# Uneven first pieces in the mixing groups and other places for the second blocks of feed-forward slabs, in one decoder layer on one core

## The chip, the cores and the metric

The kernel runs on one core of a Trainium2 chip, as one program. The metric is the device time of one execution in microseconds. Of its engines, TensorE does the matrix products (a weight load, LDWEIGHTS, and a MATMUL for each), VectorE (DVE), ScalarE (ACT) and GpSimd (POOL) work on slabs in SBUF, and SyncE (SP) issues most of the transfers. Three executions of the kernel before took 2538.45, 2538.80 and 2538.89 us, a median of 2538.8 us.

## The reference

One layer of a hybrid decoder for a prompt of 2048 tokens and for eight samples of eight tokens, all with 1024 features and the same weights. In short:

```python
def mixer(h, pos, s_ret, s_hg, w_in, ret_norm_w, hgrn_norm_w, lb, w_out):
    proj = h @ w_in                       # 1024 -> 8 * 512
    rq, rk, rv, rg, hq, hf, hi, hg = jnp.split(proj, idx, axis=-1)
    ...                                   # rotary; 4 retention heads, 4 HGRN2 heads, chunkwise
    o_r, s_ret_new = chunk_gla(rq, rk, rv, log_g_ret, s_ret)
    o_h, s_hg_new = chunk_gla(hq, k_in, v_in, log_f, s_hg)
    o = jnp.concatenate([gated(o_r), gated(o_h)], axis=-1)
    return o @ w_out, s_ret_new, s_hg_new

x = x + mixer(rmsnorm(x, norm_mix_w), ...)
h = rmsnorm(x, norm_ffn_w)
x = x + jnp.square(jax.nn.relu(h @ w_up)) @ w_down   # 1024 -> 4096 -> 1024
y = rmsnorm(x, final_norm_w)
```

Outputs are y for prompt and samples and the states of both kinds of heads.

## The kernel before

Activations lie with features on the 128 partitions and tokens along the columns. The 2112 tokens are worked off in three **mixing groups** of 640, 768 and 704 columns (`GROUPS`, L42; the last one holds the 64 sample tokens) and then in three **feed-forward groups** of 704 columns (`feed_groups`).

Every large product is made of three matmuls: weights and activations are split in a high and a low part, and hi*hi, hi*lo and lo*hi are added up in PSUM. All these matmuls are issued by the helper `matmul` (L1365 is its line). It also counts columns and drives a clock of "ticks" by them: other work (splitting weights, norms, the recurrences) is put on an agenda at a number of ticks, and is written out between the matmuls where its tick comes. A scheduler then orders the instructions of each engine by readiness and priority.

A PSUM bank holds 512 columns of float32, so a group of more than 512 columns is cut in two **pieces**, `g.pieces`. In a mixing group, `proj` goes through the weight blocks and issues, for each of the three products, one matmul for each piece, both with the same weights: first piece, second piece, first piece, and so on. So do `first_pair` for the first two projections of the kernel and `out_part` (through `proj`) for the first half of the output projection. The pieces are also the units in which results leave PSUM: `normed` (L784), `swapped` (L797, L798) and `evacuated` (L804) copy piece by piece on ScalarE, and the rotary products (L864) run on VectorE. `halves`, `parts` and `both_sums` split a slab of squares piece by piece and add it over the partitions with the weights `ones_r` (L594, L595). `parts` puts high and low part into one slab when twice the length fits into 768 columns, and takes another slab for the low part otherwise. The values (`values`) use the weights as moving operand, 256 columns at a time, and don't depend on pieces.

SBUF **slabs** are 768 columns of float32 (3072 bytes a partition) each, 49 of them in a pool. In the feed-forward stage a slab often holds two blocks of 352 columns (two rows of blocks of a half group); `pair` gives the view of it, with the second block at column 384. `out_proj` writes pairs from whole slabs of heads that are cut in two pieces of 352 columns; `up_quad` (the first eighth), `up` (seven Strassen-like products for each further eighth) and `down` read pairs as moving operand. In `up` and `down` three matmuls use one block, then three the other; in `up_quad` six and six. Pairs are also read and written by the splits (`halve`, L1409 and L1413), the sums (L1420, L1557, L1629), the squares (L1499 to L1504), the scaling of the residual and the final norm, and by transfers to and from DRAM.

The matmuls of a mixing group are interleaved with small ones of the recurrences (L992 to L1250). In a feed-forward group long runs of L1365 stand without anything between them.

Of the kernel before, what the change touches and what calls it, by code (L numbers as in the profile page):

```python
# [30 lines left out]
LAG = 14  # L31
SOON = None
SLAB = 768
NSLAB = 49
NLD = 4
NRAW, NFRAW = 4, 9
# [158 lines left out]
class Kernel:  # L195
# [25 lines left out]
    def get(self, dt=F32):  # L221
        return self.sl.tile([P, SLAB], dt, tag="slab", name="slab")

# [5 lines left out]
    def load(self):  # L229
        return self.ld.tile([P, SLAB], F32, tag="ld", name="ld")  # L230

# [199 lines left out]
    def build(self):  # L431
        nc, tc, I = self.nc, self.tc, self.I
        with ExitStack() as ctx:
            cp = ctx.enter_context(tc.tile_pool(name="cp", bufs=1))
            self.wp = ctx.enter_context(tc.tile_pool(name="wp", bufs=3))
            self.sl = ctx.enter_context(tc.tile_pool(name="sl", bufs=NSLAB))
            self.ld = ctx.enter_context(tc.tile_pool(name="ld", bufs=NLD))
# [30 lines left out]
    def groups(self, sizes):  # L468
        gs, off = [], 0
        for ns, p0, n in sizes:  # L470
            g = type("G", (), {})()
            g.i, g.ns, g.p0, g.n, g.T, g.off = len(gs), ns, p0, n, ns + n, off
            g.raw_oc, g.sources = {}, [(g, slice(0, g.T), slice(0, g.T))]
            off += g.T
            nch = n // C
            first = nch // 2
            g.pieces = [(0, g.T)] if g.T <= 512 else [(0, g.T // 2), (g.T // 2, g.T)]
            g.segs = [list(range(first)), list(range(first, nch))]
            gs.append(g)
        return gs  # L480
# [103 lines left out]
    def parts(self, src, n):  # L584

        t, half = self.getr(), SLAB // 2
        hi, lo = t[:, :n], t[:, half:half + n] if 2 * n <= SLAB else self.getr()[:, :n]
        self.nc.scalar.copy(hi, src)
# [280 lines left out]
    def values(self, g, p, b):  # L869
# [7 lines left out]
        for i0 in range(0, len(g.starts), 4):  # L877
            part = g.starts[i0:i0 + 4]
            pj = [self.bank() for _ in range(0, len(part), 2)]
            vs = [self.get() for _ in range(0, len(part), 2)]  # L880
            for i, s in enumerate(part):
                cut = slice(i % 2 * 256, i % 2 * 256 + 256)
                for kb in range(KB):
                    hh, hl = g.h[kb]
                    cols = slice((kb % 4) * 256, (kb % 4 + 1) * 256)
                    wh, wl = w[kb // 4][0][:, cols], w[kb // 4][1][:, cols]
                    for q, (a, ww) in enumerate(((hh, wh), (hh, wl), (hl, wh))):
                        self.matmul(pj[i // 2][:, cut], a[:, s:s + C], ww, start=kb == 0 and q == 0,
                                    stop=kb == KB - 1 and q == 2)
                v = vs[i // 2]  # L890
                pair = (v[:, cut.start:cut.start + P], v[:, cut.start + P:cut.stop])
                if g.ns and s == 0:
                    b["vs"], b["vrows"] = pair, v[:NS, :2 * P]
                else:
                    b["vc"].append(pair)
                if g.post:
                    with self.soon():
                        nc.scalar.activation(v[:, cut], pj[i // 2][:, cut], AF.Copy, scale=g.rc[:, i0 + i:i0 + i + 1])  # L898
                elif i % 2 or i == len(part) - 1:
                    with self.soon():  # L900
                        nc.scalar.copy(v[:, :cut.stop], pj[i // 2][:, :cut.stop])
# [457 lines left out]

    def pair(self, g, slab):  # L1360

        return slab.rearrange("p (i t) -> p i t", i=2)[:, :, :g.T // 2]

    def matmul(self, out, w, a, **k):
        self.nc.tensor.matmul(out, w, a, **k)  # L1365
# [477 lines left out]
```

## Time and profile before

| | before |
|---|---|
| median of three executions | 2538.8 us |
| profiled execution | 2538.88 us |
| its span, first to last instruction | 2537.1 us |
| TensorE matmul busy | 2506.2 us (99%) |
| VectorE busy | 1856.9 us (73%) |
| ScalarE busy | 1224.3 us (48%) |
| granted TensorE clock | 0.999 |
| read from / written to HBM | 390.62 / 138.67 MB |

The profile is of one execution. A busy share is the union of the records of an engine; a matmul's record reaches from its start to a modelled end, and records of matmuls that follow each other overlap. How fast a run of matmuls goes is therefore read from the starts: the length of an unbroken run over the number of its matmuls. The chain of work that ended last lists such runs with start, length and count. Mixing takes the first 1120 us or so of the span, the three feed-forward groups the rest, about 480 us each.

### The profile page before, as it was taken

The page shows a single profiled execution, that of the slowest core. Times are in us where ns is not written, and L with a number is a line of the kernel's source. Part 1 is how long each engine was busy: PE and PEld are TensorE (multiplying, and loading weights), DVE is VectorE, ACT ScalarE, POOL GpSimd, SP SyncE. Part 2 cuts the span into 40 slices and gives each one's busy share as a digit, 9 for nine tenths or more (in the row PEclk, how much of TensorE's full clock was granted, in tenths as well). Part 3 has the DMA queues.
Part 4 walks back from the last instruction along what each step waited for, and adds up shares of the span by engine and source line. Part 5 has one row for each costly group of instructions (what it writes and reads, how often), then busy time and mean ns, then how long its engine had stood idle before and what let it go on. Part 6 is the DMA issues. An engine that isn't in the chain of part 4 may idle for free.

```text
span 2537.1 us, 41661 instructions
## 1 busy us (share of the span) xinstructions
PE 2506.2 (99%) x16605; PEld 2480.6 (98%) x16605; DVE 1856.9 (73%) x2750; ACT 1224.3 (48%) x1769; POOL 25.1 (1%) x42
## 2 busy tenths in 40 slices
PE   8999999999999999999999999999999999999998
PEld 8999999999999999989999999999999999999998
DVE  7668866677867766656757996766699866658987
ACT  6556554345534344426444543554454445445544
POOL 0000000000000000000000000000000000000000
PEclk9999999999999999999999999999999999999999
DMA  6466685779798735484657664466766554667652
GB/s 213 150 202 235 229 295 186 237 260 313 261 338 303 267 120 172 156 297 143 195 185 255 225 204 159 152 200 184 226 230 215 175 194 154 185 193 238 206 180 70
DMA packets 209731, 532.83 MB, mean 210 GB/s; under 512 B 20736, under 2 KB 95232, under 8 KB 209536
## 3 DMA queue, kind: packets, MB, share of 16 engines
q1 hardware_dynamic: 209392, 530.14, 62.7%
q8 instruction: 131, 2.15, 0.3%
q14 instruction: 64, 0.52, 0.1%
q10 hardware_dynamic: 144, 0.02, 0.0%
HBM read 390.62 MB, written 138.67 MB: 209 GB/s over the span
## 4 chain that ended last, share of the span: by engine, by line
PE 93%; DMA 3%; DVE 3%; ACT 1%; issue 1%; SPq 0%; DVEq 0%; ACTq 0%
PE pj L1365 84%; PE mm L1062 2%; PE po L1244 1%; PE mm L1250 1%; PE mm L1119 1%; PE po L1242 1%; PE mm L595 1%; DMA raw<-w 1%; PE mm L594 1%; PE mm L1176 1%; PE po L933 1%; PE mm L992 0%; DVE slab L1023 0%; DMA s68S<-raw 0%; DMA slab<-x 0%
## 5 line engine op out<-in xcount | busy, mean ns | idle before, releaser
L1365 PE MATMUL pj<-slab,w 128*128 128x352 f32 (+2 forms) x12696 | 2115.4, 324 | 11.4 <-ACT w L648 6.5
L1365 PEld LDWEIGHTS pj<-slab,w 128*128 128x128 f32 x12696 | 2037.2, 188 | 16.3 <-ACT w L648 6.8
L338 ACT CAST w<-raw 128x1024 fp32r<-128x1024 f32 x373 | 390.7, 1048 | 620.0 <-PE pj L1365 537.1
L360 DVE TENSOR_TENSOR w<-raw,w 128x1024 fp32r<-128x1024 f32 x373 | 454.9, 1222 | 118.5 <-ACT w L338 105.7
L1365 PE MATMUL pj<-w,slab 128*128 128x256 f32 x1632 | 225.9, 288 | 0.1
L1413 DVE TENSOR_TENSOR slab<-slab 128x704 fp32r<-128x704 f32 x216 | 187.5, 885 | 32.0 <-ACT slab L1409 28.3
L1409 ACT CAST slab<-slab 128x704 fp32r<-128x704 f32 x216 | 163.6, 779 | 92.8 <-DVE slab L1420 85.8
L1365 PEld LDWEIGHTS pj<-w,slab 128*128 128x128 f32 x1632 | 205.6, 190 | 2.1 <-ACT slab L898 0.5
L1629 DVE TENSOR_TENSOR slab<-pj,slab 128x704 f32<-128x704 f32 x166 | 146.9, 888 | 65.3 <-PE pj L1365 62.7
L296 DVE TENSOR_TENSOR raw<-raw 128x1024 f32<-128x1024 f32 x60 | 73.4, 1223 | 54.6 <-DMA raw<-w 49.6
L1420 DVE TENSOR_TENSOR slab<-slab 128x704 f32<-128x704 f32 x120 | 103.6, 885 | 0.0
L1557 DVE TENSOR_TENSOR ld<-pj,slab 128x704 f32<-128x704 f32 x63 | 56.1, 890 | 55.2 <-PE pj L1365 54.9
L1043 ACT ACTIVATE slab<-slab 128x640 f32<-128x640 f32 (+2 forms) x72 | 56.2, 780 | 70.6 <-DVE slab L1039 70.2
L1557 DVE TENSOR_TENSOR slab<-pj,slab 128x704 f32<-128x704 f32 x42 | 37.4, 891 | 66.5 <-PE pj L1365 66.5
L1063 DVE COPY_PREDICATED AT<-msk,mm 128x256 f32<-128x256 uint8 (+1 forms) x72 | 38.8, 543 | 40.6 <-PE mm L1062 31.7
L413 ACT CAST slab<-slab 128x704 fp32r<-128x704 f32 (+2 forms) x48 | 36.9, 777 | 39.2 <-DMA slab<-o 16.9
L419 ACT ACTIVATE slab<-mm,eps 128x384 f32<-128x384 f32 (+3 forms) x54 | 29.5, 550 | 53.4 <-PE mm L595 50.4
L1062 PE MATMUL mm<-slab 128*128 128x128 f32 x384 | 54.1, 274 | 0.0
L1062 PEld LDWEIGHTS mm<-slab 128*128 128x128 f32 x384 | 51.1, 191 | 0.0
L1244 PE MATMUL po<-slab,S 128*128 128x128 f32 x240 | 46.3, 279 | 4.3 <-DVE S L1257 4.2
L784 ACT COPY slab<-pj 128x384 f32<-128x384 f32 (+1 forms) x64 | 26.7, 466 | 47.1 <-PE pj L1365 45.0
L1327 ACT ACTIVATE slab<-po 128x384 f32<-128x384 f32 (+2 forms) x48 | 22.0, 458 | 53.3 <-PE po L1244 53.2
(187 smaller groups left out, 1988.1 us busy)
## 6 DMA issues: line engine op xcount, KB each, us to landing
raw<-w SPq DMA_DIRECT2D x253, 512.0 KB, 4.1
u<-ld SPq DMA_DIRECT2D x96, 352.0 KB, 4.3
slab<-u SPq DMA_DIRECT2D x96, 352.0 KB, 5.2
y<-slab SPq DMA_DIRECT2D x20, 352.0 KB, 2.8
ld<-x SPq DMA_DIRECT2D x16, 384.0 KB, 6.2
raw<-s44S SPq DMA_DIRECT2D x12, 512.0 KB, 3.8
raw<-s48S SPq DMA_DIRECT2D x12, 512.0 KB, 4.4
raw<-s52S SPq DMA_DIRECT2D x12, 512.0 KB, 3.6
```

Source lines behind the costliest of these rows:

```text
L296: nc.vector.tensor_tensor(out=x[into], in0=x[a], in1=x[b], op=op)
L338: self.nc.scalar.copy(hi, raw)
L360: self.nc.vector.tensor_tensor(out=lo, in0=raw, in1=hi.bitcast(F32), op=ALU.subtract)
L1043: nc.scalar.activation(x["dd", w][:, a:T], x["dd", w][:, a:T], AF.Exp)
L1062: nc.tensor.matmul(ps[:, j * P:(j + 1) * P], qk[:, cols[c]], qk[:, cols[c]], start=True, stop=True)
L1244: nc.tensor.matmul(dst, S, qd[:, cols[c]], start=False, stop=True)
L1365: self.nc.tensor.matmul(out, w, a, **k)
L1409: self.nc.scalar.copy(self.pair(g, hi), self.pair(g, B[name]))
L1413: self.nc.vector.tensor_tensor(out=self.pair(g, lo), in0=self.pair(g, B[name]), in1=self.pair(g, hi).bitcast(F32), op=ALU.subtract)
L1420: self.nc.vector.tensor_tensor(out=self.pair(g, s), in0=self.pair(g, B[a]), in1=self.pair(g, B[b]), op=op)
L1557: nc.vector.tensor_tensor(out=b2(out), in0=ps, in1=b2(s), op=ALU.add)
L1629: nc.vector.tensor_tensor(out=r, in0=ps, in1=r, op=ALU.add)
```

## The change

Two tables of three numbers. The first piece of a mixing group is no longer half of it: 304 of 640, 400 of 768, 336 of 704 columns, so the second piece has 336, 368 and 368. And the second block of a pair slab stands at column 368 in the first feed-forward group, 360 in the second and 376 in the third, where it stood at 384 in all. The blocks stay 352 columns long. The pieces of `out_proj` are made in `feed_groups` and stay halves.

```diff
 SLAB = 768
+FIRST_PIECE = (304, 400, 336)
+SECOND_BLOCK = (368, 360, 376)
 NSLAB = 49
...
-            g.pieces = [(0, g.T)] if g.T <= 512 else [(0, g.T // 2), (g.T // 2, g.T)]
+            g.pieces = [(0, FIRST_PIECE[g.i]), (FIRST_PIECE[g.i], g.T)]
...
     def pair(self, g, slab):
 
-        return slab.rearrange("p (i t) -> p i t", i=2)[:, :, :g.T // 2]
+        return slab[:, :2 * SECOND_BLOCK[g.i]].rearrange("p (i t) -> p i t", i=2)[:, :, :g.T // 2]
```

The lines of the changed kernel stand two further down than before (L1365 is L1367 there). On TensorE in the third mixing group, between the recurrences of its third head, there stood before (line, operation, out<-in, partitions x columns, count):

```order
L594 MATMUL mm<-slab,ones_r 128x320
L595 MATMUL mm<-slab,ones_r 128x320
L1365 MATMUL pj<-slab,w 128x352 x6
L992 MATMUL mm<-con,slab 128x128 x2
L1365 MATMUL pj<-slab,w 128x352 x2
```

and now, on the same engine at the same place:

```order
L596 MATMUL mm<-slab,ones_r 128x320
L597 MATMUL mm<-slab,ones_r 128x320
L1367 MATMUL pj<-slab,w 128x368
L1367 MATMUL pj<-slab,w 128x336
L1367 MATMUL pj<-slab,w 128x368
L1367 MATMUL pj<-slab,w 128x336
L1367 MATMUL pj<-slab,w 128x368
L994 MATMUL mm<-con,slab 128x128 x2
```

The equal halves of 352 columns have become pieces of 336 and 368 in turn, and the small matmuls between them have moved by a matmul or so. On TensorE in the first feed-forward group, from the last sums of the mixing stage on, there stands now:

```order
L597 MATMUL mm<-slab,ones_r 128x384 x2
L1367 MATMUL pj<-slab,w 128x352 x812
L596 MATMUL pj<-slab,ones_r 128x352
L597 MATMUL pj<-slab,ones_r 128x352
L1367 MATMUL pj<-slab,w 128x352 x20
```

It stood there before in the same order and number (with L594, L595 and L1365), and so it does to the end of the program: in the feed-forward groups only the addresses are others. On VectorE, where the second mixing group's squares are split (L589, now L591) while the first group's heads are worked on, there stood before:

```order
L1254 COPY S<-mm 128x128 x2
L589 TENSOR_TENSOR slab<-slab 128x384 x2
L1257 SCALAR_TENSOR_TENSOR S<-S,mm 128x128
L864 TENSOR_TENSOR slab<-pj,slab 128x320
L1257 SCALAR_TENSOR_TENSOR S<-S,slab,mm 128x128
L864 TENSOR_TENSOR slab<-pj,slab 128x320
```

and now:

```order
L1256 COPY S<-mm 128x128 x2
L591 TENSOR_TENSOR slab<-slab 128x400
L1259 SCALAR_TENSOR_TENSOR S<-S,mm 128x128
L591 TENSOR_TENSOR slab<-slab 128x368
L866 TENSOR_TENSOR slab<-pj,slab 128x304
L1259 SCALAR_TENSOR_TENSOR S<-S,slab,mm 128x128
L866 TENSOR_TENSOR slab<-pj,slab 128x336
```

The state update S now stands between the two halves of the split, one place earlier.

## The prediction

> **What bounds the kernel now.** I read the page first: the span, the busy shares, and who makes up the chain that ended last.
>
> ```profile
> span 2537.1 us, 41661 instructions
> ...
> PE 2506.2 (99%) x16605; PEld 2480.6 (98%) x16605; DVE 1856.9 (73%) x2750; ACT 1224.3 (48%) x1769; POOL 25.1 (1%) x42
> ...
> PE 93%; DMA 3%; DVE 3%; ACT 1%; issue 1%; SPq 0%; DVEq 0%; ACTq 0%
> ```
>
> TensorE is the bound: 99% busy, 93% of the chain. The profiled execution took 2538.88 us, 1.8 us more than its span and within 0.1 us of the median of 2538.8; I sum against 2538.88. Next, the list of what TensorE waited for (us in total, times, longest):
>
> ```profile
> PE pj L1365 <- ACT w L648: 6.5, 2, 5.8
> PE po L1244 <- DVE S L1257: 4.2, 6, 2.0
> PE pj L1365 <- DVE slab L1660: 2.5, 2, 1.5
> ...
> PE mm L594 <- DVE slab L589: 0.5, 1, 0.5
> ```
>
> These waits are small, and the largest, on L648, is the kernel's first weights. So the time is set by how closely the matmuls of L1365 follow each other. The groups by shape give the counts:
>
> ```profile
> L1365 PE MATMUL pj<-slab,w 128*128 128x352 f32 x10056 | 1644.3, 324 | 2.6 <-DVE slab L1660 2.5
> ...
> L1365 PE MATMUL pj<-slab,w 128*128 128x384 f32 x1344 | 257.3, 340 | 1.2 <-DMA w<-w32lo 1.0 <-DMA w<-w16lo 0.2
> ```
>
> The 324 ns is the length of one record; the records overlap, so it is not the pace. The pace comes from the chain in order of time, whose rows give start, length and count of an unbroken run:
>
> ```profile
> 356.01 31.03 PE pj L1365 x179
> ...
> 751.03 25.38 PE pj L1365 x157
> ...
> 1119.84 130.93 PE pj L1365 x812
> 1254.61 346.39 PE pj L1365 x2164
> 1603.99 115.67 PE pj L1365 x716
> 1723.50 346.39 PE pj L1365 x2164
> 2072.89 115.67 PE pj L1365 x716
> 2192.40 323.52 PE pj L1365 x2022
> ```
>
> At 384 columns (second mixing group) one matmul takes 31.03/179 = 173.3 ns. At 352 columns there are **two paces**: 323.52/2022 = 160.0 ns and 346.39/2164 = 160.1 ns in the bulk of the feed-forward groups, but 25.38/157 = 161.7 ns in the third mixing group and 130.93/812 = 161.2 ns at the start of the first feed-forward group (115.67/716 = 161.6 in the next two, short waits included). One clean run of the first mixing group, from the timeline (start, length to the end of its last record, count):
>
> ```profile
> 24.19 7.20 PE L1365 MATMUL mm<-slab,w 128*128 128x320 f32 x48
> ```
>
> Less the last record (0.31 us) over 47 steps that is 146.6 ns at 320 columns. So 146.6, 160.0, 173.3 ns: 0.417 ns a column and a fixed 13.3 ns (160.0 - 352 x 0.417).
>
> **The cuts, by the slope.** A pair of pieces costs 0.417 ns times the group's columns plus twice 13.3 ns, wherever the cut lies: 304+336 = 640, 400+368 = 768, 336+368 = 704. As lengths the new pieces cost nothing. The Trainium skill's page "TensorE: Matmul & The Clock Gate", section "Back-to-back issue gap", gives the isolated warm gap as N/2.4 + 2.5 ns, 149.2 ns at 352 columns (an estimate by that page). The slope agrees with the trace, the fixed part is smaller than the 13.3 ns here; an uneven cut sums to zero by either.
>
> **The starts.** What is left of the change is where a matmul's moving operand begins. In bytes from the slab's start, the second pieces begin now at 1280, 1536 and 1408: multiples of 256 in the first two groups, 128 past one in the third. The slow 161.7 ns belongs to the third. The feed-forward pair slabs have their second block at 1536, a multiple again, and run at 160.0; but each group opens with `out_proj`, which uses whole slabs cut at 352 columns (1408 bytes), and there the slow pace returns. It then outlasts `out_proj`. The timeline shows where it ends in the first group:
>
> ```profile
> 1250.44 0.32 PE L1365 MATMUL pj<-slab,w 128*128 128x352 f32 x1
> 1250.60 0.32 PE L594 MATMUL pj<-slab,ones_r 128*128 128x352 f32 x1
> 1250.76 0.32 PE L595 MATMUL pj<-slab,ones_r 128*128 128x352 f32 x1
> 1250.92 3.20 PE L1365 MATMUL pj<-slab,w 128*128 128x352 f32 x19
> ```
>
> Two column sums with other weights break the run; behind them 19 matmuls take (3.20 - 0.32)/18 = 160.0 ns each. So I read the slow pace as a pattern in TensorE's own stream, set up where consecutive starts stand 128 bytes apart modulo 256, and kept until something breaks it. That is an inference: no matmul of L1365 in this trace starts anywhere else.
>
> - Third mixing group: as many matmuls as the second, x1344. The second piece moves from 1408 to 1344 bytes, out of the 128-byte relation. At the fast pace: 1344 x (161.66 - 160.0) = **-2.2 us**.
> - Feed-forward, the stretches at 161 ns: 812 + 716 + 716 = 2244 matmuls, less 192 of `out_proj` in each group (8 outputs x 4 units x 3 products x 2 halves), whose cut stays at 352: 1668. With the second block at 1472, 1440 or 1504 bytes I expect the pattern not to be carried on: 1668 x 1.24 = **-2.1 us**.
> - The stretches at 160.0 ns of the feed-forward and the first two mixing groups: no row shows their new starts. Ends: below, nothing excludes a gain of up to the fixed 13.3 ns a matmul; above, the slow pace, +1.66 ns. The nearest row is the 160.0 of the same instructions. I take 0.
>
> **The other engines.** They work on the same columns at other places:
>
> ```profile
> L1413 DVE TENSOR_TENSOR slab<-slab 128x704 fp32r<-128x704 f32 x216 | 187.5, 885 | 32.0 <-ACT slab L1409 28.3 <-PE pj L1365 3.2
> ...
> L414 DVE TENSOR_TENSOR slab<-slab 128x704 fp32r<-128x704 f32 x24 | 21.0, 886 | 4.3 <-ACT slab L413 4.3
> ...
> L784 ACT COPY slab<-pj 128x384 f32<-128x384 f32 x32 | 13.7, 479 | 20.7 <-PE pj L1365 19.6 <-PE po L1242 1.0
> ...
> L784 ACT COPY slab<-pj 128x352 f32<-128x352 f32 x32 | 13.0, 453 | 26.4 <-PE pj L1365 25.4 <-PE po L1242 1.0
> ```
>
> L1413 works on two blocks with a gap between them, L414 on whole slabs: 885 and 886 ns, so the gap's size costs VectorE nothing. ScalarE's L784 copies one piece out of PSUM at (479 - 453)/32 = 0.8 ns a column: 13 ns more for the longer piece, 13 less for the shorter. It hides in the idle time ahead of L784, 20.7 and 26.4 us over 32 copies each, nearly all of it waiting for TensorE; uncovered it would be 13 ns a pair. One edge: in the second group `parts` no longer fits twice 400 columns into one slab of 768 and takes another of the 49. If that made a wait, it would be at the sums behind L589, where TensorE waits 0.5 us now; I take 0, and 0.5 as its end. The scheduler moves a few small matmuls and copies by some places in the mixing groups; with the waits as short as above I give this 0, +-2 us.
>
> Sum: 2538.88 - 2.2 - 2.1 = **2534.6 us**.
>
> **Rivals.**
>
> *Starts don't matter (2538.9).* The pattern may belong to the length 352 with alternating PSUM banks, or to what precedes, and come back whatever the address. For it: the first feed-forward run stays slow long after `out_proj`, with starts that are fast later. Against it: 320 and 384 columns alternate banks too and show 146.6 and 173.3. The third group would have to stay at 161.7 as an average. The Trainium skill's page "SBUF — State Buffer", section "Who interferes with whom", says this too: TensorE has separate read ports for moving operand and weight load and never waits on anyone. The two paces of one shape, 160.0 and 161.2, are something that rule leaves out.
>
> *The pattern spreads (2550).* Now almost all matmuls start at multiples of 256 bytes; afterwards nearly every stream alternates between such a start and another one: first and second piece in all mixing groups, first and second block in the feed-forward. The one alternating stream in the trace is the slow one. If any alternation makes it: feed-forward stretches at 160.0, 2164 + 2164 + 2022 = 6350 x 1.66 = 10.5 us, first two mixing groups 2688 x 1.66 = 4.5 us, +15.0 in all; if only each changeover counts, which comes every third matmul in the feed-forward and every one in mixing, 3.5 + 4.5 = +8.0. I take the middle, 11.5: 2550.4. It makes the kernel measurably slower from 5.1/9038 = 0.56 ns a matmul on. Against it: the moves are by 32 to 96 bytes from a multiple of 256, not by 128.
>
> *The fixed 13.3 ns shrinks (2514.6).* If part of it comes from weights and moving operand starting alike, a moved start saves some. Moved starts: 3 x 672 second pieces and half of the feed-forward's pair matmuls ((192 + 1176 + 1344)/2 = 1356 a group, by the loops of `up_quad`, `up` and `down`), 6084. At all of the 13.3 ns that is 81 us; no row gives a size, and I take 4 ns, nearer to nothing: 24.3 us. Against it, a stream with other weights in the timeline:
>
> ```profile
> 750.69 0.33 PE L595 MATMUL mm<-slab,ones_r 128*128 128x384 f32 x1
> 750.87 25.38 PE L1365 MATMUL pj<-slab,w 128*128 128x352 f32 x156
> ```
>
> 0.18 us from one to the next at 384 columns: no shorter than 173.3 ns.
>
> **How the numbers follow.** About 0.2% (5.1 us) is what a measurement of this kernel can tell from no change. Forecast 0.36, starts don't matter 0.15, the pattern spreads 0.27, the fixed part shrinks 0.22. The forecast of -4.3 us, +-2 for the scheduler, lies inside the 0.2% more often than outside: 0.22 within, 0.14 faster. Faster is 0.14 + 0.22 = 0.36, same 0.22 + 0.15 = 0.37, slower 0.27. The range reaches from 2514 (the middle of the shrinking case; its further half, some 0.1, is left out) to 2552 (the dearer third of the spreading case left out). The likeliest case alone is 2532 to 2537.
>
> **What would show it.** In the chain after, the pace of the unbroken runs says all: the third mixing group's pairs at 320.0 ns instead of 323.3; the 812 and 716 runs ending faster, with the three long runs still at 160.0 (forecast); the long runs at 161 or more (spread), or below 160, and then by group, since each group has another block start (shrink). I am wrong at the root if the paces stay and the waits of TensorE change.

## The result, and the profile after

| | before | after |
|---|---|---|
| median of 18 executions each | 2538.8 us | 2542.4 us |
| ratio to before, 95% interval | | 1.0015 (1.0008 to 1.0022) |
| profiled execution / span | 2538.88 / 2537.1 us | 2543.25 / 2541.5 us |
| start of feed-forward (run x812) | 1119.84 us | 1118.71 us |
| feed-forward: start of x812 to end of x2022 | 1396.08 us | 1401.50 us |

The kernel became 0.15% slower, 3.6 us by the medians and 4.4 us by the spans. The forecast was 4.2 us faster. First the head of the page of the changed kernel, and the largest entries of its list of what TensorE waited for (us in total, times, longest):

```profile
span 2541.5 us, 41664 instructions
...
PE 2512.1 (99%) x16605; PEld 2487.5 (98%) x16605; DVE 1856.2 (73%) x2750; ACT 1221.3 (48%) x1767; POOL 25.5 (1%) x42
```

```profile
PE pj L1367 <- ACT w L650: 5.9, 1, 5.9
PE pj L1367 <- DVE slab L1662: 2.5, 2, 1.5
PE po L1246 <- DVE S L1259: 2.5, 5, 0.8
```

VectorE and ScalarE are as busy as before, and the waits are not longer in sum. One has grown by more than 0.5 us, that of L597 on L416 in the mixing groups, from 0.6 to 2.0 us; L1246 on S (L1244 before) fell by more, from 4.2 to 2.5 us. TensorE is 5.9 us busier with the same 16605 matmuls. The chain of the changed kernel in order of time (start, length, what, count) shows where:

```profile
355.29 31.16 PE pj L1367 x179
...
750.90 25.14 PE pj L1367 x157
...
1118.71 131.17 PE pj L1367 x812
1253.75 349.83 PE pj L1367 x2164
1606.58 115.57 PE pj L1367 x716
1726.02 348.69 PE pj L1367 x2164
2077.70 115.15 PE pj L1367 x716
2196.69 323.52 PE pj L1367 x2022
```

Row by row against before:

- Second mixing group (400 and 368): 31.16/179 = 174.1 ns instead of 173.3. Times 1344: **+1.0 us**.
- Third mixing group (336 and 368): 25.14/157 = 160.1 ns instead of 161.7: **-2.1 us**. Together -1.1 us. Both take the pace of one long run for a whole group. Over all steps from one matmul of L1365 to the next with nothing between them (some 1170 and 1130 in each trace) the means go from 173.9 to 174.3 ns and from 161.5 to 160.3 ns: +0.5 and -1.6 us, again -1.1 together. The feed-forward does start 1.1 us earlier, but that the two agree so well is luck, as its start varies by more from one execution to the next (below).
- The runs x812, x716, x716: +0.24, -0.10, -0.52, **-0.4 us** in all.
- The long runs: block at 368 **+3.44** (161.7 ns), at 360 **+2.30** (161.1 ns), at 376 **0.00** (160.0 ns).

-1.1 - 0.4 + 5.7 = 4.2 of the 4.4 us. Nearly all of it is two long runs in which each step from one matmul to the next is 1.1 or 1.6 ns longer than it was, with nothing waited for. In the same stretch of before the steps between the starts are 160 ns each; with the block at 368 they go from 155 to 171 ns.

### The profile page after: what moved, and what is told of

It reads as the page before. It is cut to its first block, busy times and chain, and to the rows that moved or that the text cites. A ratio compares the mean times of both kernels' runs of the same rounds, so it can differ in the third digit from the quotient of the medians.

```text
span 2541.5 us, 41664 instructions
## 1 busy us (share of the span) xinstructions
PE 2512.1 (99%) x16605; PEld 2487.5 (98%) x16605; DVE 1856.2 (73%) x2750; ACT 1221.3 (48%) x1767; POOL 25.5 (1%) x42
## 4 chain that ended last, share of the span: by engine, by line
PE 92%; DMA 3%; DVE 2%; ACT 1%; issue 1%; SPq 0%; DVEq 0%; ACTq 0%
PE pj L1367 83%; PE mm L1064 1%; PE po L1246 1%; PE mm L1252 1%; PE po L1244 1%; DMA raw<-w 1%; PE mm L1121 1%; PE mm L597 1%; PE mm L596 1%; DMA slab<-x 1%; PE mm L1178 1%; DMA s44S<-raw 1%; PE mm L994 0%; PE po L935 0%; DVE slab L1025 0%
## 5 line engine op out<-in xcount | busy, mean ns | idle before, releaser
L1367 PE MATMUL pj<-slab,w 128*128 128x352 f32 (+4 forms) x12696 | 2121.8, 325 | 10.3 <-ACT w L650 5.9
L1367 PEld LDWEIGHTS pj<-slab,w 128*128 128x128 f32 x12696 | 2044.0, 188 | 14.6 <-ACT w L650 5.9
L1367 PE MATMUL pj<-w,slab 128*128 128x256 f32 x1632 | 225.4, 288 | 0.0
L1367 PEld LDWEIGHTS pj<-w,slab 128*128 128x128 f32 x1632 | 205.4, 190 | 1.5 <-ACT slab L900 0.2
L421 ACT ACTIVATE slab<-mm,eps 128x384 f32<-128x384 f32 (+6 forms) x54 | 29.4, 551 | 54.0 <-PE mm L597 51.0
L786 ACT COPY slab<-pj 128x400 f32<-128x400 f32 (+1 forms) x64 | 26.7, 466 | 49.7 <-PE pj L1367 47.7
L1246 PE MATMUL po<-slab,S 128*128 128x128 f32 x240 | 46.5, 280 | 2.5 <-DVE S L1259 2.5
L799 ACT COPY slab<-pj 64x368 f32<-64x368 f32 (+3 forms) x44 | 19.9, 452 | 59.2 <-PE pj L1367 40.8
```

Source lines behind the costliest of these rows:

```text
L1246: nc.tensor.matmul(dst, S, qd[:, cols[c]], start=False, stop=True)
```

## The experiments

The start of the feed-forward differs by up to 4.4 us between executions of one kernel (1116.72 and 1121.16 us, below), so kernels are compared by the paces and by the **length of the feed-forward**, from the start of x812 to the end of x2022. This length repeats to 0.02 us in the two kernels that were profiled twice. The lines of the layer's kernels below are those of before. Paces are lengths over counts.

### One part at a time

Pieces only:

```diff
-SLAB = 768
+SLAB = 768; FIRST_PIECE = (304, 400, 336)
...
-            g.pieces = [(0, g.T)] if g.T <= 512 else [(0, g.T // 2), (g.T // 2, g.T)]
+            g.pieces = [(0, FIRST_PIECE[g.i]), (FIRST_PIECE[g.i], g.T)]
```

> The uneven first pieces alone; the second blocks of the feed-forward stay at column 384. Theory A (the loss sits in the feed-forward and comes from the place of the second block; the cuts gain a little): the long runs x2164, x2164, x2022 stay at 346.4, 346.4 and 323.5 us (160.0 ns a matmul), the third mixing group's x47 runs go from 7.60 to 7.53 us, and the feed-forward starts about 1.1 us earlier: 2537.7 us, ratio 0.9993 to 0.9998. Theory B (the uneven cuts leave a state behind that the feed-forward inherits): the first long run is at about 349.8 us here too, and the time 2541 to 2543 us. Theory C (the gain ahead of the feed-forward in the one profile was chance): feed-forward starts at 1119.8 us, ratio 1.0000.

Blocks only:

```diff
-SLAB = 768
+SLAB = 768; SECOND_BLOCK = (368, 360, 376)
...
-        return slab.rearrange("p (i t) -> p i t", i=2)[:, :, :g.T // 2]
+        return slab[:, :2 * SECOND_BLOCK[g.i]].rearrange("p (i t) -> p i t", i=2)[:, :, :g.T // 2]
```

> The second blocks at 368, 360, 376 alone; the mixing groups are cut in halves as before. Theory A (place of the second block): x2164 at 349.8 us, x2164 at 348.7 us, x2022 at 323.5 us, feed-forward starts at 1119.8 us as before, 2543.6 to 2544.2 us, ratio 1.0019 to 1.0022: slower than with both parts. Theory B (inherited from uneven cuts): all three long runs at 160.0 ns, 2538.8 us.

The long runs, from the chain of the kernel with the blocks only:

```profile
1252.69 349.83 PE pj L1365 x2164
...
1724.96 348.69 PE pj L1365 x2164
...
2195.63 323.52 PE pj L1365 x2022
```

Those are the lengths of the full change. Feed-forward: 1401.59 us with the blocks alone, 1396.08 with the pieces alone, to the hundredth that of before. The ratios: pieces 0.9992 (0.9984 to 1.0001), blocks 1.0023 (1.0013 to 1.0034). Theory A holds: the blocks lose, and nothing is inherited from the cuts across the stages. That the cuts gain about 1 us is worked out from the paces; the ratio of the pieces alone doesn't tell it from nothing.

### Other places

The second block at six more columns, by the same table, with a view that can also begin past 384:

```diff
-        return slab.rearrange("p (i t) -> p i t", i=2)[:, :, :g.T // 2]
+        v = slab.rearrange("p (i t) -> p i t", i=2)[:, :, :g.T // 2]; return bass.AP(v.tensor, v.offset, [list(v.ap[0]), [SECOND_BLOCK[g.i], 2], list(v.ap[2])])
```

> Second blocks at columns 352, 392, 400 in the three feed-forward groups: 128 bytes before, 32 after and 64 after the multiple of 256 at which they stood; cuts as before. Theory A1 (the distance between the two blocks modulo 256 bytes counts, either sign alike): 352 like out_proj, 161.2 to 161.7 ns a matmul, x2164 at 349 to 350 us; 392 like 376, 160.0 ns, x2164 at 346.4 us; 400 like 368, about 161.6 ns, x2022 at 326 to 327 us. Theory A2 (the block's own place against something fixed counts, such as where weights begin): the sign matters, so 392 and 376 or 400 and 368 differ by over 1 ns. Theory A3 (any second block below its old place by over 32 bytes is slow, above is not): 352 slow, 392 and 400 at 160.0 ns.

> Second blocks at columns 408, 416, 380: 96 after, 128 after and 16 before the multiple of 256. Theory A1 (distance modulo 256 bytes, either sign alike): 408 like 360, about 161.1 ns a matmul, x2164 at 348.7 us; 416 like 352, 161.2 to 161.7 ns, x2164 at 349 to 350 us; 380 at 160.0 ns, x2022 at 323.5 us. Theory A2 (the block's own place against something fixed): 408 or 416 differ from 360 and 352 by over 1 ns, or 380 isn't at 160.0. Theory A3 (only places below): 408 and 416 at 160.0 ns, 346.4 us each.

The long runs of the second of these, 408, 416 and 380:

```profile
1255.24 349.85 PE pj L1365 x2164
...
1726.39 344.09 PE pj L1365 x2164
...
2192.23 323.53 PE pj L1365 x2022
```

161.7, **159.0** and 160.0 ns. The first gave 348.70 (352: 161.1), 346.39 (392: 160.0) and 325.76 us (400: 161.1). Theory A1 falls: 352 and 416 are both 128 bytes from a multiple of 256, one slow, one faster than anything before. A3 falls too, as 400 and 408 lie above and are slow. A2 stays. So far, however, group and place were always changed together.

### Group or place, distance or start

The places of the change in other groups: `SECOND_BLOCK = (360, 376, 368)`.

> Second blocks at 360, 376, 368: the places of the change, each in another group. Theory P (place decides): first group 161.1 ns, x2164 at 348.7 us; second group 160.0 ns, 346.4 us; third group 161.7 ns, x2022 at 326.9 us. Theory G (group or what precedes decides): first group 161.7 ns (349.8 us), second 161.1 (348.7 us), third 160.0 (323.5 us), as with the change.

Measured: 348.69, 346.39 and 326.88 us, what Theory P named. 360, 376 and 368 take their paces along into another group. The same question for 416, in a kernel meant as an improvement (`FIRST_PIECE = (320, 384, 336)`, `SECOND_BLOCK = (416, 416, 416)`):

> First pieces 320, 384, 336 (only the third group is cut unevenly) and second blocks at column 416 in all three feed-forward groups. Theory P (the pace is a property of the block's place): 416 was 159.0 ns a matmul in the second group and is so in all: x2164 at 344.1, x2164 at 344.1, x2022 at 321.4 to 321.5 us, the runs of 812 and 716 about 1 us shorter each, the feed-forward starts 1.4 us earlier: 2526 to 2529 us, ratio 0.9950 to 0.9965. Theory I (the pace is inherited from what runs ahead of it, and the 159.0 ns belonged to the second group): only the second group gains, 2535 to 2537 us, and the first or third can be at 161.

```profile
1250.80 348.70 PE pj L1365 x2164
...
1721.32 348.70 PE pj L1365 x2164
...
2191.34 321.27 PE pj L1365 x2022
```

Both theories miss: 161.1, 161.1 and 158.9 ns for one place, and by the starts of the matmuls the stretches of up ahead of the first two run at a third pace, 160.0. So 416 has **three steady paces**, and something other than place and group number picks one. The ratio is 0.9988 (0.9976 to 0.9999). Then both blocks moved alike, `FIRST_BLOCK` added to the view's offset:

> Both blocks moved by the same amount, 16, 32 and 8 columns, so that they stay 384 apart: (16, 400), (32, 416), (8, 392). Theory D (only the distance between the two blocks counts): 346.4, 346.4 and 323.5 us, 160.0 ns as before. Theory W (the place against the weights' start counts): the first two groups leave 160.0 ns by 1 ns or more either way, 344.1 or 348.7 us and up.

```profile
1252.48 346.09 PE pj L1365 x2164
1601.57 119.11 PE pj L1365 x716
1724.48 342.94 PE pj L1365 x2164
...
2189.25 323.52 PE pj L1365 x2022
```

With (32, 416) the long run goes at 342.94/2164 = 158.5 ns, and the run of 716 just ahead of it, with the same blocks from up_quad on, at 166.4 on average. Theory D falls: the distance is 384 in both. Theory W was half right, since (16, 400) stays at 160.0, as does (8, 392) in the third group.

### What picks the pace

Two more matmuls with other weights, as a break between up_quad and up, put into the kernel before and into the changed one:

```diff
-        g.B = None
+        g.B = None; self.column_sums(self.bank2()[:, 0, :g.T // 2], *(self.pair(g, s)[:, 0] for s in g.ops[1]["T4"]))
```

> The kernel before with one pair of column sums more (two matmuls with other weights, result unused) between up_quad and the first up of each feed-forward group. Theory I (the 161.1 ns in up is a pattern carried on from out_proj and up_quad, and ends at any break): the 428 and twice 332 matmuls of up that ran at 161.1 ns run at 160.0, 1.2 us less in all, the long runs stay at 160.0; with the six sums themselves (6 x 0.16 us = 1.0 us) the time is 2538.5 to 2539 us. Rival (those stretches are slow for another reason, or a break starts the slow pattern as well as it ends it): the stretches stay at 161.1 ns, or the long runs of some group go to 161.1 (348.7 us): 2540 us or more.

> The changed kernel with one pair of column sums more (result unused) between up_quad and the first up of each feed-forward group. If the slow pattern at 368 and 360 is one of several that a break can end: at least one of the runs of 428 (or their counterparts) or the long runs in the first two groups goes to 160.0 ns or below. If 368 and 360 have only the slow one: up stays at 161.7 (69.2 us for 428) and 161.1 ns (69.0 us), the long runs at 349.8 and 348.7, third group 323.5 us; 2544 us.

The stretch of up behind the break, kernel before with the sums, groups one to three:

```profile
1183.39 68.48 PE pj L1365 x428
...
1652.14 68.96 PE pj L1365 x428
...
2121.39 68.48 PE pj L1365 x428
```

In the first and third group the break ends the slow pattern (68.48/428 = 160.0 ns), in the second it does not (161.1). The order of the matmuls and the columns at which they begin are the same in all three (which slabs they use was not compared), so a break can end the slow pattern or leave it. Feed-forward: 1396.12 us, nothing gained. In the changed kernel the break changes nothing at 368 and 360 (69.19 and 68.95 us, the long runs again 349.83 and 348.69), and at 376 it brought the slow pattern in: 68.95 us in the third group, 1403.02 us in all. In this sense a break draws a pattern anew.

Whether the draw differs from execution to execution was asked with unchanged kernels:

> The changed kernel once more. If 368, 360 and 376 have one pattern each, whatever the execution: x2164 at 349.8, x2164 at 348.7, x2022 at 323.5 us again. If they inherit one of several: another pace in at least one of them, 346.4 or 344.1 us for instance.

> The kernel of pieces_416 once more, unchanged. Its twelve times spread over 18 us, those of the kernel before over 6. Theory I (which of several steady patterns a group falls into is set by the few ns ahead of its last break and so differs from execution to execution): at least one of x2164, x2164, x2022 is at another pace than last time (161.1, 161.1, 158.9 ns), but each again at one of 158.9, 160.0 or 161.1 ns. Theory P2 (pace fixed by place, group and preceding code): 348.7, 348.7, 321.3 us again.

The changed kernel gave 349.83, 348.69 and 323.52 us again; the one with 416 gave 348.70, 348.70 and 321.27. So in these profiles the program fixes the draw, and Theory I as it stood for these runs falls. The twelve times of the kernel with 416 reach from 2528.7 to 2547.0 us, against 2536.2 to 2541.9 for before; its two profiles differ only ahead of the feed-forward. Where the timed executions differ isn't seen and stays open.

### Where the pattern of before comes from

The prediction had `out_proj` set it up. Here `out_proj` reads heads laid out in blocks at 0 and 384 as well, so that nothing in a feed-forward group begins elsewhere (`FIRST_PIECE = (320, 384, 336)` beside it):

```diff
-                    self.matmul(ps, w, a[:, c0:c1], start=j == 0 and q == 0, stop=j == n - 1 and q == 2)
+                    self.matmul(ps, w, a[:, c0 + g.gap * (c0 > 0):c1 + g.gap * (c0 > 0)], start=j == 0 and q == 0, stop=j == n - 1 and q == 2)
...
-        self.cut(g.raw_oc.pop((p, hd)), hi, lo, g.T, 2)
+        s = g.raw_oc.pop((p, hd)); self.cut(*((s[:, :g.T].rearrange("p (i t) -> p i t", i=2), self.pair(g, hi), self.pair(g, lo), 2) if g.gap else (s, hi, lo, g.T)), 2)
```

> First pieces 320, 384, 336, second blocks at 384 as before, and the heads that out_proj reads are laid out in two blocks too, the second at column 384, so that every moving operand of a feed-forward group begins at column 0 or 384. Theory I (the 161 ns of out_proj's whole slabs is what up_quad and the first up inherit): no cause is left, the runs x812, x716, x716 go near 160.0 ns, 130.0, 114.6 and 114.6 us and less, 2 to 3 us in all, the long runs stay at 346.4, 346.4, 323.5; with 1.4 us from the third mixing group 2534.5 to 2536 us, ratio 0.9980 to 0.9990. Rival (the slow pattern can start by itself at 384 too, or comes from the mixing stage): the runs of 812 and 716 stay at 161 ns, 2537 to 2538 us.

```profile
1118.47 130.82 PE pj L1365 x812
...
1602.36 115.63 PE pj L1365 x716
...
2071.06 115.63 PE pj L1365 x716
```

Before they were 130.93, 115.67 and 115.67. In the first group `out_proj` runs at 161.1 ns from its start, by the starts of its matmuls (161.7 before). In the second and third its first 96 matmuls follow `down` without a wait, at the end of the run of 2164, and keep the 160.0 ns of that run. The other 96 come behind a wait, at the head of the run of 716, and go at 161.1, as `up_quad` and `up` do after them. In the second group, on the two sides of the wait (timeline: start, length to the end of the last record, count):

```profile
1585.76 13.44 PE L1365 MATMUL pj<-slab,w 128*128 128x352 f32 x83
...
1603.28 12.89 PE L1365 MATMUL pj<-slab,w 128*128 128x352 f32 x79
```

Less the last record that is (13.44 - 0.32)/82 = 160.0 and (12.89 - 0.32)/78 = 161.2 ns, for the same instruction on blocks at the same columns. So the slow pattern can begin by itself at 0 and 384, within `out_proj`. The rival holds. The ratio, 0.9990 (0.9981 to 0.9999), includes the third mixing group.

### The streams alone

A program that leaves out the layer and has streams only, with TensorE alone at work: the transfers of its data end within the first 50 us, and VectorE is busy for 1% of the span, between streams. Its core is the loop of up. `w` is by how many columns the weights are moved, `f` and `s` are the columns of the two blocks, `WB` and `SB` where weights and slabs begin, and `P` is 128:

```python
hi = WB + w + 2048 * (r % 2)
for i in range(2):
    for kb in range(4):
        a = SB + 1536 * (kb // 2) + (s if kb % 2 else f)
        c = i * 512 + kb * P
        for j, (wo, ao) in enumerate(((hi, a), (hi, a + 768), (hi + 1024, a))):
            yield ps[:m, i, :n], self.w[:, wo + c:wo + c + m], self.s[:, ao:ao + n], kb == j == 0, kb == 3 and j == 2
```

> All of the layer's computation is left out (outputs hold input columns). 58 short streams run in a row, each of 48 + 144 matmuls in the order of up (three with one block, three with the other, weights 128 columns further every third), 352 columns, slabs and weights placed as in the kernel, no other engine at work. Read is the length of the run of 144. Streams: second block at 352 to 416 in steps of 8, each entered three ways (after a wait of TensorE and two column sums; straight from out_proj's order; from that order and two column sums); weights moved by 16 to 96 columns; both blocks moved by 16 to 64, with and without the weights; weight tiles of 64 and 32 columns; 128, 256, 320 moving columns. Theory R (starts of the blocks against the weights' start decide which steady patterns there are, the entry picks one): 384 at 160.0 or 161.1 ns (23.0 or 23.2 us), by entry; 368 and 408 at 161.7 (23.3 us) by every entry; 416 at 158.9, 160.0 or 161.1; blocks moved alone leave 160.0 (158.3 or 166.7 at 32), weights moved alone too, all moved alike give 160.0. Theory D (only the blocks' distance counts): moving weights or both blocks changes nothing. Theory E (other engines' accesses to SBUF make it): one pace everywhere. If the fixed 13.3 ns is the reading of 128 weight columns, 64 give about 153.3 ns and 32 about 150.0; otherwise 160.0.

Its chain, the runs of 144 with the block at 368 and 384, entered after a wait; then weights moved by 32 and 96 columns, both blocks moved by 32, and all moved by 32:

```profile
122.91 23.30 PE pj L290 x144
...
187.22 23.05 PE pj L290 x144
...
1077.53 22.82 PE pj L290 x144
...
1173.38 24.01 PE pj L290 x144
...
1270.03 22.81 PE pj L290 x144
1301.72 23.05 PE pj L290 x144
```

161.8, 160.1, 158.5, 166.7, 158.4 and 160.1 ns. An entry is what runs just ahead of a stream. By the three entries (a wait and two sums; matmuls in out_proj's order; these and two sums), in ns:

| second block | 352 | 360 | 368 | 376 | 384 | 392 | 400 | 408 | 416 |
|---|---|---|---|---|---|---|---|---|---|
| wait | 161.2 | 161.2 | 161.8 | 161.2 | 160.1 | 160.1 | 161.2 | 161.7 | 160.0 |
| straight | 160.0 | 161.1 | 161.7 | 160.0 | 161.1 | 160.0 | 161.1 | 161.7 | 161.1 |
| sums | 160.0 | 161.1 | 161.7 | 161.1 | 160.0 | 162.2 | 161.1 | 161.7 | 160.1 |

Theory E falls: the paces are there with no other engine at work. D falls: moved weights alone give 158.5 or 166.7 ns. R holds in the main: 360, 368, 400 and 408 are slow by every entry, the others have two or more paces; moved together by 32, blocks and weights are at 160.1 again, by 48 and 64 at 161.2, the other pace of 384.

The grid crosses weight places, block places and entries:

> All of the layer's computation is left out (outputs hold input columns). 216 streams as in bench_starts, each of 48 matmuls to settle and 48 that are read (7.68 us at 160.0 ns): the weights moved by 0 to 112 columns in steps of 16, for each of them the second block at 352 to 416 in steps of 8, for each of these the three entries (wait and sums; straight from out_proj's order; that order and sums). Theory R (the starts against the weights' start fix the set of steady patterns, the entry picks among them): unmoved weights repeat bench_starts, 360 and 400 at 161.1, 368 and 408 at 161.7 ns by every entry (7.73 and 7.76 us), 352, 376, 384, 392, 416 at one of 158.9, 160.0, 161.1, 162.2; at least one pair of weight place and block place gives less than 160.0 ns by all three entries, and weights moved by 96 with the block at 384 give 166.7 or 158.3 ns by entry. Theory N (entry alone decides, places only change the phase at which the entry arrives): in every place both fast and slow paces turn up among the three entries, and no place is fast or slow by all three in more than about a quarter of the cases.

The runs that are read, weights moved by 16 columns and the block at 384, by the three entries, and then weights moved by 32:

```profile
866.70 7.68 PE pj L277 x48
...
889.82 7.68 PE pj L277 x48
...
913.26 7.70 PE pj L277 x48
...
1436.75 8.00 PE pj L277 x48
...
1460.10 7.60 PE pj L277 x48
...
1483.78 8.01 PE pj L277 x48
```

160.0, 160.0 and 160.4, then 166.7, 158.3 and 166.9. The paces repeat when the weights move by 64 columns (256 bytes) in 33 of 36 places; in the other three at least one entry draws otherwise. Theory R holds, Theory N falls: of the 36 places with weights moved by less than 64 columns, 26 have one pace by all three entries, and 360, 368, 400 and 408 are as slow as in the first program. R's hope of a place that is below 160.0 by all entries isn't met; the best are places with 160.0 alone, such as weights 16 or 48 columns past with blocks 384 apart. One pace by all three entries is no proof that there is no other: at 376 it is 161.2 by all three here, 160.0 by all three with the weights 64 columns on, and both in the first program.

### A place with one pattern

Weights 48 columns past the blocks modulo 64 is the same as blocks 16 past the weights. So all blocks of the feed-forward, those of the heads too (laid out as above), go to columns 16 and 400, with cuts of 320, 384 and 336:

```diff
+SLAB = 768; FIRST_PIECE = (320, 384, 336); FIRST_BLOCK = (16, 16, 16); SECOND_BLOCK = (400, 400, 400)
...
+        v = slab.rearrange("p (i t) -> p i t", i=2)[:, :, :g.T // 2]; return bass.AP(v.tensor, v.offset + FIRST_BLOCK[g.i], [list(v.ap[0]), [SECOND_BLOCK[g.i] - FIRST_BLOCK[g.i], 2], list(v.ap[2])])
```

> First pieces 320, 384, 336; in the feed-forward groups all blocks at columns 16 and 400, and the heads that out_proj reads laid out in such blocks too. Theory R (the grid: weights 48 columns past, which is the same relation as blocks 16 columns past modulo 64, and blocks 384 apart run at 160.0 ns by all three entries): no stretch of a feed-forward group is slow, whatever comes ahead: x812, x716, x716 at 130.0, 114.6 and 114.6 us and no more, x2164, x2164, x2022 at 346.2 to 346.4, same, 323.5; with 1.4 us from the third mixing group 2534 to 2535 us, ratio 0.9978 to 0.9986, and the times of single executions spread no wider than those of the kernel before. Rival (in the full kernel something else brings the slow pattern up): the runs of 812 and 716 stay at 161 ns as in heads_384, 2536 to 2537 us.

```profile
1119.77 129.92 PE pj L1365 x812
1253.53 346.24 PE pj L1365 x2164
1602.77 114.83 PE pj L1365 x716
1721.44 346.24 PE pj L1365 x2164
2070.68 114.83 PE pj L1365 x716
2189.35 323.52 PE pj L1365 x2022
```

No stretch of the feed-forward is slow: it takes 1393.10 us, 2.98 less than before and 8.4 less than with the change. The paces are those that Theory R named. The median is 2535.8 us against 2539.0 for before beside it, ratio 0.9988 (0.9978 to 0.9997): faster than before, by a little less than was expected. No run has it beside the changed kernel. The ratio alone doesn't single this place out, as the cut of the third mixing group is in it and the kernels with 416 and with the heads at 384 came to 0.9988 and 0.9990; the length of the feed-forward does (1395.89 and 1395.58 us in those two). Its times spread over 6.1 us, those of before over 5.3: a little wider, where no wider was expected.

## Why the prediction was wrong

- **What bounds the kernel, and the pace as its measure:** right. All of the loss is pace; waits and other engines stayed nearly as they were, as forecast, and the wait on L591 is 0.5 us also with the 400 columns that no longer fit two to a slab.
- **Third mixing group, -2.2 us:** right, -2.1 by the long run and -1.6 by all steps. The **second group**, taken at 0 because its old start was a good one, lost 1.0 or, by all steps, 0.5: 400 with 368 is slower than 384 with 384.
- **Feed-forward stretches at 161 ns, -2.1 us:** wrong, -0.4. I expected that a new start would end the pattern. Only at 376 did `up` go to 160.0 ns. At 368 and 360 every entry that was tried leads to a slow one, in two groups of the kernel each, behind the extra sums, and with the streams alone. And the pattern was not the doing of the cut at 352: without it, behind a wait, the pattern began at 384. The term's count was off as well: in the second and third group the first 96 matmuls of `out_proj` end the long runs, so 1860 matmuls were left, not 1668. They ran at 161.1 ns and not at the mean of 161.24, so that the two errors cancel: 1860 x 1.1 is 2.1 us too.
- **Stretches at 160.0 ns, "I take 0":** this is the step that failed, by 5.7 us. I had bounded it above by the slow pace, +1.66 ns a matmul, and that is what 368 took; but I chose the nearest row, the same instructions at their old starts, which says nothing of new ones. The trace had shown one thing about other starts, that the stream which used them was slow.
- **Rivals.** "The pattern spreads" had the sign and the mechanism (+8.0 or +15.0 us); its condition was wrong. Alternation as such doesn't make it: 376, 380 and 392 alternate with a multiple of 256 bytes at 160.0, and (32, 416), where both blocks stand alike, has 166.4. What counts, besides what ran ahead, is each start against the weights' start modulo 256 bytes, which the two blocks and the weights set together. "Starts don't matter" is refuted by the rotated places. Of "the fixed 13.3 ns shrinks" there is a trace: 158.3 to 159.0 ns exist, 1.7 ns at most and not by every entry.
- **Ports.** With no other engine at work the places alone make 158.3 to 166.7 ns. The Trainium skill's page "SBUF — State Buffer", section "Who interferes with whom", gives TensorE separate ports for moving operand and weight load and has it never wait on anyone. As far as other engines go the streams alone agree, since they show the paces of the layer; what the two streams of TensorE itself do to its pace is something that the rule leaves out.

What is not settled: why these relations are slow. That the reads of moving operand and weights meet in SBUF would fit the 256-byte period, but it is not shown: no run looked inside a matmul. What exactly a break leaves behind that picks a pattern is open too.

## What to carry to other kernels

Where TensorE is full, read its pace from unbroken runs in the chain: 1.6 ns a matmul, invisible in busy shares and waits, was worth 3.4 us in one run. The place in SBUF of an operand is a tuning parameter with its own measurement: run the bare stream at each place and with several things ahead of it, and take a place with one pace by all of them, rather than the fastest seen once; then read the paces again in the kernel, since a few entries don't show every pace. Rows at the old places bound nothing at new ones.

## What the runs showed of the hardware that was not expected

- A steady stream of one shape has up to three paces that last for hundreds of matmuls: 158.9, 160.0 and 161.1 ns at 416; 158.3 and 166.7 ns at (32, 416).
- Weight tiles of 64 columns gave 22.73/144 = 157.8 ns a matmul, of 32 columns 160.1, by one entry each: the fixed 13.3 ns doesn't shrink with the weights' columns.
- Moving operands of 320 and 256 columns gave 146.7 and 120.1 ns, on the slope of the prediction; 128 columns gave 16.09/144 = 111.7 ns, far above the 66.7 of that slope, so at 128 columns something else sets the pace.
